# A two-layer decoder trunk in split fp32: normalisation of the second half of queries and keys without priority, three raw weight buffers in place of four, transposes of the attention two matmuls further apart

## The chip, the cores and the metric

The kernel runs on one core of one Trainium2 chip. The metric is the device time of one execution in microseconds (us); lower is better. Traces are of one profiled execution each.

In what follows PE is the matmul engine (its weight loads are listed as PEld), DVE the vector engine, ACT the scalar engine, POOL the general engine, and SP the engine that here only issues transfers. The work of one engine runs in the order in which its instructions stand in its stream. The transfers that SP issues stand in one queue as well: an instruction of SP that waits holds back all later ones.

## The reference

Input is x, 512 tokens by 2048 columns in fp32. Two residual layers follow, each `x <- x + W_out(mixer(rms_norm(x)) * silu(gate))`, both with one wide input projection.

```python
# layer 0: differential attention, 8 heads, each with 2 x 128 query and key columns, 256 value columns
q, k, v, gate = split(rms_norm(x) @ w_in)
q, k = rope(rms_norm(q, q_gain)), rope(rms_norm(k, k_gain))
p = softmax(where(causal, q @ k.T * dh ** -0.5, neg))     # for both halves of a head
o = (p[0] - lam * p[1]) @ v
out = (rms_norm(o, subln_w) * (1 - lambda_init) * silu(gate)) @ w_out

# layer 1: RWKV-7, 32 heads of 64 columns, r, k, v, gate, decay and in-context rate a from one projection
S = S * w_t + (S @ a_t) b_t^T + v_t k_t^T                 # along the 512 tokens
y_t = S @ r_t                                            # then group norm, gate, w_out
```

## The kernel before

Every large product is computed as three products of halves: `split_w` makes from a raw fp32 weight tile a rounded part `wh` (a cast on ACT, line 105) and the rest `wl` (a subtraction on DVE, line 106), and the activations lie as `hH` and `hL`. A raw tile is 128 partitions by two row blocks of 512 columns, 512 KB. It is loaded by SP (line 78) into the pool `wraw` of four buffers that rotate; the pools `wh` and `wl` have two buffers each.

**Layer 0.** Head 0 projects its 1024 columns plainly. Heads 1 to 7 go through `unit_head`, which computes the 2 x 2 block product of a head by seven block products on sums of blocks, in groups of 12 matmuls of 512 columns (line 565), one raw tile for a group. A product has four groups. Four of the raw tiles of a head lie in tiles of their own, `Ta` to `Td`, and are loaded by `first_tiles` while the head before still runs; the other four come through `load` (line 545) into `wraw`, first the lower rows of the query and key columns, then those of the value columns. POOL adds other quarters of the weights to these tiles by accumulating transfers (`add_w`).

When a head's projections for a half of the tokens are there, `head_qk` treats the query and key columns of two token tiles: squares on ACT (line 261), then on DVE two rotary products (269, 270), the sum of squares (271), the cosine product (272), the sum (273), at the end of both tiles the inverse root (274 and lines 64 to 71), and the scaling of the keys by four small ACT instructions (line 280). `take` (line 527) adds a product to what is accumulated. The transposes into `qkT` and `qkL` follow on PE (`turn_qk`, line 295). The half [0, 1] comes in the middle of a head. The half [2, 3] comes at its end and stands inside `high_priority(offset=AHEAD)`.

Attention of head h-1 runs among the matmuls of head h. A `Chain` is a generator; each yielded number says after how many matmuls its next step is put in (`tick`). `attention` yields 8 after scores and weighing, and gap - 8 after transposes: `turn` transposes the probabilities (line 363), `turn_y` transposes the head's output into `yTh` and `yTl` (line 400), which ACT's queue stores to `ys` for the output projection. For head 0 a chain of its own transposes the queries and keys, with a delay of 104 matmuls.

**Layer 1.** There are 16 pairs of heads with one pattern. For each pair k, gate, r and v are projected (two raw tiles each, 24 matmuls a tile, line 122), and two small matrices come into `upw`, a ninth tile of the pool `wraw` (lines 1565 and 1566), split into `sHup` (1098) and `sLup` (1099). A triangular solve on DVE (lines 1353 and 1355) gives `Tm`, POOL stores it to `td` (1357), SP reads it back rearranged into `TT` by four transfers (line 1370), DVE transposes it (1379), and the `px` matmuls (1385, 1395) and the Gram matmuls (1288) follow on PE. The scan of the pair before runs between the projection matmuls.

**Who sets the order.** A tile scheduler places each engine's instructions by priority, the order of the program with the offsets of `high_priority`; `split_w` is itself urgent. Waits come from the data and from the rotation of buffers. A load into `wraw` waits until the `wl` of that buffer's last user has been computed.

Of the kernel before, what the change touches and what calls it, by code (L numbers as in the profile page):

```python
# [57 lines left out]
def rsqrt(g, out, v, n, tag):  # L58

    nc = g.nc  # L60
    m = 1 if tag in ("r4", "r16") else 2
    sh = g.small.tile([P, n], I32, name="rs_i", tag=tag + "i", bufs=m)
    t = g.small.tile([P, n], F32, name="rs_t", tag=tag + "t", bufs=m)
    nc.vector.tensor_single_scalar(sh[:], v.bitcast(I32), 1, ALU.logical_shift_right)
    nc.vector.tensor_scalar(sh[:], sh[:], -1.0, float(0x5F3759DF), ALU.mult, ALU.add)
    y = sh[:].bitcast(F32)
    for i in range(3):
        nc.vector.tensor_mul(t[:], y, y)
        nc.vector.scalar_tensor_tensor(t[:], t[:], -0.5, v, ALU.mult, ALU.mult)
        o = out if i == 2 else y  # L70
        nc.vector.scalar_tensor_tensor(o, t[:], 1.5, y, ALU.add, ALU.mult)
# [254 lines left out]
def attention(g, h, qkT, qkL, sq, V, VL, G, gap, rows=None, keys=()):  # L326
# [87 lines left out]
    for i in range(NT + 3):  # L414
        if i > 1 and i < NT + 2:
            weigh(i - 2)
        if i > 2:
            turn_y(i - 3)
        if i < NT + 2:
            yield 8  # L420
        while due:
            store(*due.pop())
        if i == NT + 2:
            break
        if 0 < i <= NT:
            turn(i - 1)
        if i < NT:
            scores(i)
        if i == 0 and keys:
            yield 7  # L430
            turn_qk(*keys[0])
            yield 9
            turn_qk(*keys[1])
            yield max(gap - 24, 6)
        else:
            yield gap - 8
    if rows is not None:
        rows += last

# [90 lines left out]
def unit_head(g, aps, h, t1s, sq, turned):  # L530


    nc = g.nc
    c1, c2 = qk_cols(aps, h), vg_cols(aps, h)
    acc1 = g.work.tile([P, 2, 512], F32, name="acc1", tag="acc1", bufs=1)
    acc = [None, None, acc1[:, 0], acc1[:, 1]]
    q = [t[:] for t in t1s]
    N = NH4 // KG
    last = h == NH - 1

    def pair():
        return [g.pp.tile([P, 512], F32, name="pp", tag="pp") for _ in range(2)]

    def load(k0, parts):
        raw = g.wraw.tile([P, KG, 512], F32, name="wraw", tag="wraw")
        load_w(g, raw, parts, k0, slice(0, KG))
        return raw

    def split(raw):
        return split_w(g, None, KG, 512, 0, raw)  # L550

    def block(k0, t0):
        return lambda k, t: [x[k0 + k][:, t0 + t * P : t0 + (t + 1) * P] for x in (g.hH, g.hL)]

    def form(nm, i):
        return lambda k, t: [x[:, t * P : (t + 1) * P] for x in g.sums[nm][i * KG + k]]

    def products(out, lhs, raw, start=False, end=False):
        wt = split(raw)
        for t in range(2):  # L560
            first = start
            for lo in range(2):
                for k in range(KG):
                    for x in lhs(k, t)[: 2 - lo]:
                        m = nc.tensor.matmul(out[t][:], x, wt[lo][:, k, :], start=first, stop=end and lo == 1 and k == KG - 1,  # L565
                                             skip_group_check=True)
                        tick(g, m)
                        first = False

    def all_groups(out, lhs, raw, start=False, end=False, then=None):  # L570
        for i in range(N):
            r = raw(i)
            products(out, lhs(i), r, start and i == 0, end and i == N - 1)
            if then:
                add_w(g, r, then[0], then[1] + i * KG)

    def s4(out, keep, start=False, end=False):
        def raw(i):
            keep.append(load(NH4 + i * KG, c2))
            return keep[-1]  # L580
        all_groups(out, lambda i: form("S4", i), raw, start, end, None if last else (c2, 0))

    chained = lambda i: g.Ts[i]
    y = pair()
    all_groups(y, lambda i: block(NH4 + i * KG, 0), lambda i: load(NH4 + i * KG, c1), True, True)
    copy_out(g, q[:2], y)
    y = pair()
    all_groups(y, lambda i: block(i * KG, 0), chained, True, False, (c2, 0))
    take(g, q[:2], y)
    X = pair()  # L590
    all_groups(X, lambda i: form("S1", i), chained, True, last, (c2, NH4))
    copy_out(g, acc[2:], X)
    b22 = []
    if not last:
        s4(X, b22, end=True)
        G, acc[:2] = gates(g)
        copy_out(g, acc[:2], X)
    all_groups(y, lambda i: form("S2", i), chained, then=(c1, NH4))
    if last:
        G, acc[:2] = gates(g)  # L600
    take(g, acc[:2], y, ALU.subtract, acc[2:] if last else None)

    def square():
        X = pair()
        all_groups(X, lambda i: block(NH4 + i * KG, 256), chained, True, True)
        return X

    def third():
        for i in range(N):
            if last:  # L610
                b22.append(load(NH4 + i * KG, c2))
                add_w(g, b22[i], c2, i * KG)
            products(y, form("S3", i), b22[i], end=i == N - 1)
        take(g, acc[2:], y, ALU.subtract)

    head_qk(g, t1s, sq, [0, 1])
    if last:
        copy_out(g, q[2:], square())
        third()
        take(g, q[2:], y)  # L620
        with g.tc.high_priority(offset=AHEAD):
            head_qk(g, t1s, sq, [2, 3])
        turned()
        X = pair()
        s4(X, [], True, True)
        take(g, acc[:2], X)
        return head_vg(g, h, acc, G)
    turned()
    third()
    copy_out(g, q[2:], y)  # L630
    values = head_vg(g, h, acc, G)
    X = square()
    first_tiles(g, aps, h + 1)
    take(g, q[2:], X)
    with g.tc.high_priority(offset=AHEAD):
        head_qk(g, t1s, sq, [2, 3])
    return values


# [154 lines left out]
def layer0(g, aps):  # L794
# [3 lines left out]
    with ExitStack() as cx:  # L798
# [25 lines left out]
        with tc.high_priority(offset=AHEAD):  # L824
# [4 lines left out]
                first = nc.scalar.dma_start(out=g.prm_a[:], in_=aps["norm_w"]).ins  # L829
            g.last = load_w(g, g.first[0][0], qk_cols(aps, 0), 0, slice(0, 1), nc.sync)  # L830
            warmed = warm_up(10)
            on = g.const.tile([P, 1], F32, name="on")
            nc.vector.memset(on[:], 0.0)
            with tc.issue_after(first):
                nc.scalar.copy(on[:], on[:])
# [17 lines left out]
        g.last = None  # L853
        t1s = [t1_tile() for _ in range(NT)]
        copied = copy_out(g, [t[:] for t in t1s], qk0)
        sc = g.small.tile([P, NT, 4], F32, name="ssc", tag="ssc", bufs=1)
        for cb, tags in enumerate((("qkL",), ("sA2",), ("sC2",), ("qkL",))):
            n = NT // len(tags)
            xs = []
# [30 lines left out]
        for h in range(NH):  # L890
# [6 lines left out]
            def keys(n, t1s=t1s, qkT=qkT):  # L897
                for t in range(n):
                    turn_qk(g, t1s, *qkT, t)
                    if t < n - 1:  # L900
                        yield 20
# [4 lines left out]
            else:  # L906
                for ts in ([0, 1], [2, 3]):
                    head_qk(g, t1s, sq, ts)
                Chain(g, keys(NT), 104)
                input_sums(g, pairs, False)  # L910
                ps = unit_tok(g, g.hH, g.hL, vg_cols(aps, h), 512)
                acc1 = g.work.tile([P, 2, 512], F32, name="acc1", tag="acc1", bufs=1)
# [70 lines left out]
        def banks(i):  # L983
            if i < 2:
# [1 line left out]
            return [g.ps.tile([P, 512], F32, name="z", tag="pa", bufs=2) for _ in range(2)]  # L986

        T2 = g.work.tile([P, KG, 512], F32, name="T2", tag="Tb", bufs=1)
        load = loader(g, aps["da_w_out"], ((g.wraw, "wraw", 4), (g.work, "V", 1), (g.wraw, "wraw", 4),
                                              (g.work, "G", 1), (g.wraw, "wraw", 4)))  # L990

        rs = g.small.tile([P, NT], F32, name="rs1", tag="ss")
        ss = g.small.tile([P, NT], F32, name="ss1", tag="rr")
# [217 lines left out]
def stage1(g, j, k, up):  # L1211
# [14 lines left out]
    lw, tha = th  # L1226
    nc.scalar.activation(lw[:], lw[:], AF.Identity, bias=g.hdec[:], scale=-0.5 * DECAY)
    l = w.tile([P, NC_, C], F32, name="l", tag="l", bufs=1)
    m = g.small.tile([P, NC_], F32, name="m", tag="m")
    p.E = w.tile([P, NC_, C + 1], F32, name="E", tag="E", bufs=1)  # L1230
    p.gam = g.small.tile([P, NC_], F32, name="gam", tag="gam", bufs=3)
    p.AR = w.tile([P, NC_, 2, C], F32, name="AR", tag="AR", bufs=3)
# [281 lines left out]
def centre(g, p):  # L1514

    nc, w, Y = g.nc, g.work, p.Y
    s1 = g.small.tile([P, NT, 2], F32, name="s1", tag="s1")
    p.yc = w.tile([P, 2 * NT, C], F32, name="yc", tag="yc", bufs=1)
    for h in range(2):
        yg = Y[h][:, : NT * C].rearrange("p (t n) -> p t n", t=NT)  # L1520
# [6 lines left out]
def group_norm(g, j, p):  # L1527
# [2 lines left out]
    NG = 2 * NT  # L1530
    sq = w.tile([P, NG, C], F32, name="ysq", tag="thg", bufs=1)
    nc.scalar.activation(sq[:], yc[:], AF.Square)
    var = g.small.tile([P, NG], F32, name="var", tag="var")
    nc.vector.reduce_sum(var[:], sq[:], AX.X)
    nc.vector.tensor_scalar(var[:], var[:], 1.0 / C, GN_EPS, ALU.mult, ALU.add)
    rs = g.small.tile([P, NG], F32, name="rsg", tag="rsg")
    rsqrt(g, rs[:], var[:], NG, "r8")
    nc.vector.tensor_mul(yc[:], yc[:], rs[:, :, None].to_broadcast([P, NG, C]))

# [10 lines left out]
def layer1(g, aps):  # L1550
    nc, tc = g.nc, g.tc
    with ExitStack() as cx:
# [127 lines left out]
        def banks(i):  # L1680
            if i == 0:
# [4 lines left out]
        load = loader(g, aps["rw_w_out"], ((g.wraw, "wraw", 4), (w, "G1", 2), (g.wraw, "wraw", 4), (w, "LT", 1),  # L1686
                                              (g.wraw, "wraw", 4), (w, "G1", 2)))
        seven(g, aps["rw_w_out"], load, rows, sums, 2, 3, acc, Ts, banks, done)


# [1 line left out]
def body(ctx, tc, nc, aps):  # L1692
# [3 lines left out]
    g.chains, g.later, g.state = [], [], None  # L1696
    g.const = ctx.enter_context(tc.tile_pool(name="const", bufs=1))
    g.hp = ctx.enter_context(tc.tile_pool(name="hp", bufs=16))
    g.wraw = ctx.enter_context(tc.tile_pool(name="wrawp", bufs=4))
    g.wh = ctx.enter_context(tc.tile_pool(name="whp", bufs=2))  # L1700
    g.wl = ctx.enter_context(tc.tile_pool(name="wlp", bufs=2))
    g.small = ctx.enter_context(tc.tile_pool(name="small", bufs=2))
# [53 lines left out]
```

## Time and profile before

| what | us |
|---|---|
| median of three runs | 2172.89 |
| the three runs | 2160.70, 2172.89, 2174.74 |
| profiled execution, its time | 2171.03 |
| profiled execution, its span | 2169.3 |
| PE busy | 2110.7 |
| DVE busy | 1614.6 |
| ACT busy | 1149.3 |

The span runs from the first to the last instruction of the trace. Layer 0 with its output projection takes roughly the first half, up to about 1000 us, layer 1 the rest. All times inside the trace are from the start of the span. The mean granted PE clock of the profiled execution is 0.984 of full speed.

### The profile page before, as it was taken

What the parts mean: (1) busy time and instruction counts of PE and PEld (TensorE: products, weight loads), DVE (VectorE), ACT (ScalarE), POOL (GpSimd) and SP (SyncE); (2) the same over time, 40 slices, a digit from 0 to 9 for tenths busy, and PEclk for the clock granted to TensorE, in tenths of its full rate; (3) what the DMA queues carried; (4) which work ended last, traced back from release to release, by engine and by line L of the source; (5) the groups of instructions that cost most, each with busy time, mean ns of one, the idle gap of its engine ahead of it and who ended that gap; (6) DMA issues with size and microseconds to landing.
All of it is one profiled execution on the core that took longest, in us unless ns stands there. A gap on an engine that the chain in (4) does not pass through costs nothing.

```text
span 2169.3 us, 34050 instructions
## 1 busy us (share of the span) xinstructions
PE 2110.7 (97%) x11852; PEld 1711.5 (79%) x11852; DVE 1614.6 (74%) x4129; ACT 1149.3 (53%) x2278; POOL 386.2 (18%) x751
## 2 busy tenths in 40 slices
PE   9999999999998999999899999999999999999999
PEld 7787878778787788878677778888887888867887
DVE  6887888888787885566777667877776788757644
ACT  5665656566565543355554555565555555545322
POOL 1020111201113000101322222222222122221001
PEclk9999999999999999999998999999999999999999
DMA  8487877879789836623222322322332233335555
GB/s 271 131 173 186 181 159 182 163 180 178 165 186 213 300 112 184 140 87 103 77 74 63 93 81 83 91 89 78 101 102 84 82 92 90 108 111 185 179 156 120
DMA packets 143102, 294.60 MB, mean 136 GB/s; under 512 B 47969, under 2 KB 65377, under 8 KB 142929
## 3 DMA queue, kind: packets, MB, share of 16 engines
q1 hardware_dynamic: 75072, 178.55, 25.8%
q0 software_dynamic: 25216, 87.74, 21.9%
q10 hardware_dynamic: 42640, 26.14, 4.0%
q8 instruction: 93, 1.52, 0.3%
q14 instruction: 81, 0.66, 0.1%
HBM read 268.71 MB, written 23.66 MB: 135 GB/s over the span
## 4 chain that ended last, share of the span: by engine, by line
PE 49%; DVE 14%; DMA 5%; issue 3%; ACT 2%; POOL 0%; SPq 0%; ACTq 0%; POOLq 0%; DVEq 0%
PE pp L122 29%; PE pt L122 5%; PE pp L565 3%; DVE wl L106 3%; DVE tmpl L1353 2%; DMA td<-Tm 2%; DVE Tm L1355 2%; PE gp L1288 2%; DMA TT<-td 1%; PE sm L1466 1%; PE sm L1477 1%; PE px L1395 1%; PE lora L122 1%; PE px L1385 1%; ACT wh L105 1%
## 5 line engine op out<-in xcount | busy, mean ns | idle before, releaser
L106 DVE TENSOR_TENSOR wl<-wraw,wh 128x1024 fp32r<-128x1024 f32 (+2 forms) x291 | 356.1, 1224 | 230.5 <-ACT wh L105 222.3
L105 ACT CAST wh<-wraw 128x1024 fp32r<-128x1024 f32 (+2 forms) x291 | 303.5, 1043 | 328.1 <-PE pp L122 153.5
L122 PE MATMUL pp<-hH,wl 128*128 128x512 f32 x1024 | 417.4, 408 | 0.2 <-DVE wl L106 0.2
L122 PE MATMUL pp<-hL,wh 128*128 128x512 f32 x1024 | 416.3, 407 | 0.0
L122 PE MATMUL pp<-hH,wh 128*128 128x512 f32 x1024 | 415.5, 406 | 0.0
L122 PEld LDWEIGHTS pp<-hH,wh 128*128 128x128 f32 x1024 | 196.0, 191 | 36.6 <-issue 2.7
L122 PEld LDWEIGHTS pp<-hL,wh 128*128 128x128 f32 x1024 | 195.8, 191 | 35.7
L122 PEld LDWEIGHTS pp<-hH,wl 128*128 128x128 f32 x1024 | 195.4, 191 | 33.9 <-DVE wl L106 0.7
L565 PE MATMUL pp<-wh,hH 128*128 128x512 f32 x448 | 176.7, 394 | 0.1
L565 PE MATMUL pp<-wh,hL 128*128 128x512 f32 x448 | 175.8, 392 | 0.0
L565 PE MATMUL pp<-wl,hH 128*128 128x512 f32 x448 | 142.2, 397 | 9.4 <-DVE wl L106 9.4
L122 PE MATMUL pp<-wh,hH 128*128 128x512 f32 x372 | 145.8, 392 | 0.9 <-ACT hH L1089 0.9
L122 PE MATMUL pp<-wl,hH 128*128 128x512 f32 x372 | 146.0, 393 | 0.4 <-DVE wl L106 0.4
L122 PE MATMUL pp<-wh,hL 128*128 128x512 f32 x372 | 145.6, 391 | 0.1
L1472 POOL COPY SA<-VS 64x64 f32<-64x64 f32 x224 | 64.5, 288 | 450.3 <-DVE VS L1488 349.7
L1353 DVE SCALAR_TENSOR_TENSOR tmpl<-LT,Tm 128x60 f32<-128x60 f32 (+24 forms) x496 | 134.5, 271 | 11.5
L1355 DVE TENSOR_TENSOR Tm<-Tm,tmpl 128x60 f32<-128x60 f32 (+24 forms) x496 | 104.0, 210 | 10.6
L565 PEld LDWEIGHTS pp<-wl,hH 128*128 128x128 f32 x448 | 82.5, 189 | 27.8 <-DVE wl L106 11.9
L565 PEld LDWEIGHTS pp<-wh,hH 128*128 128x128 f32 x448 | 84.6, 189 | 17.7 <-issue 0.5
L565 PEld LDWEIGHTS pp<-wh,hL 128*128 128x128 f32 x448 | 84.5, 189 | 17.3
L1469 ACT COPY rhs<-sm 64x64 f32<-64x64 f32 x256 | 52.5, 205 | 74.6 <-PE sm L1466 71.9
L1479 ACT COPY VS<-sm 64x64 f32<-64x64 f32 x256 | 52.7, 206 | 59.5 <-PE sm L1477 54.0
(394 smaller groups left out, 4493.8 us busy)
## 6 DMA issues: line engine op xcount, KB each, us to landing
wraw<-in_rw_w_in_dram SPq DMA_DIRECT2D x128, 512.0 KB
wraw<-in_da_w_in_dram SPq DMA_DIRECT2D x75, 512.0 KB
wraw<-in_da_w_in_dram POOLq DMA_DIRECT2D x28, 512.0 KB, 5.8
wraw<-in_da_w_out_dram SPq DMA_DIRECT2D x26, 512.0 KB
wraw<-in_rw_w_out_dram SPq DMA_DIRECT2D x26, 512.0 KB
Ta<-in_da_w_in_dram POOLq DMA_DIRECT2D x21, 512.0 KB, 5.6
Tb<-in_da_w_in_dram POOLq DMA_DIRECT2D x21, 512.0 KB, 5.7
Tc<-in_da_w_in_dram POOLq DMA_DIRECT2D x21, 512.0 KB, 6.0
```

Of the source, the lines that this page charges most:

```text
L105: a = nc.scalar.copy(hi[:, ks], raw[:, ks])
L106: d = nc.vector.tensor_sub(lo[:, ks], raw[:, ks], hi[:, ks].bitcast(F32))
L122: m = nc.tensor.matmul(out, a, b, start=s, stop=e, skip_group_check=skip)
L565: m = nc.tensor.matmul(out[t][:], x, wt[lo][:, k, :], start=first, stop=end and lo == 1 and k == KG - 1, skip_group_check=True)
L1288: m = nc.tensor.matmul(gp[h][:, i * P : (i + 1) * P], BK[r_, c0 + i, :, :], p.AR[r_, c0 + i, :, :], start=True, stop=True)
L1353: nc.vector.scalar_tensor_tensor(tt, LT[:, i : i + 1, i + 1 :].to_broadcast([P, s, n]), n2[:, i : i + 1], Tm[:, 0:s, i : i + 1].to_broadca ...
L1355: nc.vector.tensor_add(Tm[:, 0:s, i + 1 :], Tm[:, 0:s, i + 1 :], tt)
L1385: nc.tensor.matmul(px[hi, c * HALF : (c + 1) * HALF], p.G[lo, c, 0, h, HALF:C], T1[lo, c, :], start=True, stop=True, tile_position=(b0, b0 ...
L1395: nc.tensor.matmul(px[lo, N + c * HALF : N + (c + 1) * HALF], X[hi, c, :], TT[hi, c, h, HALF:C], start=True, stop=True, tile_position=(b0 ...
L1469: nc.scalar.copy(rhs[r_, :], sm[r_, h * C : h * C + C])
L1472: nc.gpsimd.tensor_copy(p.SA[r_, c - 1, :], VS[r_, c, h, :])
L1479: nc.scalar.copy(VS[r_, c, h, :], sm[r_, P : P + C])
```

## The change

There are three parts. First, the two calls of `head_qk` for the half [2, 3] lose `high_priority(offset=AHEAD)`. Second, `wraw` has three buffers in place of four; in heads 1 to 7 of layer 0 the fourth load of a product goes to a tile `Te` of its own, so that four tiles rotate there as before. The output projections, the low-rank tiles and layer 1 have three. Some small tiles get a third buffer or another place; the room comes from the buffer that is gone. Third, `attention` yields 10 where it yielded 8, and takes two from the following gap, so that a round is as long as before; the first gap has a floor of 6 and stays at 6. The chain of head 0's keys starts after 120 matmuls in place of 104.

```diff
 def rsqrt(g, out, v, n, tag):
-    m = 1 if tag in ("r4", "r16") else 2
+    m = 1 if tag in ("r4", "r16") else 3 if tag == "r8" else 2
...
         if i < NT + 2:
-            yield 8
+            yield 10
...
             turn_qk(*keys[1])
-            yield max(gap - 24, 6)
+            yield max(gap - 26, 6)
         else:
-            yield gap - 8
+            yield gap - 10
...
-    def load(k0, parts):
-        raw = g.wraw.tile([P, KG, 512], F32, name="wraw", tag="wraw")
-        load_w(g, raw, parts, k0, slice(0, KG))
+    def load(i, k0, parts):
+        pool, tag, bufs = (g.work, "Te", 1) if i == N - 1 else (g.wraw, "wraw", 3)
+        raw = pool.tile([P, KG, 512], F32, name="wraw", tag=tag, bufs=bufs)
+        load_w(g, raw, parts, k0 + i * KG, slice(0, KG))
         return raw
...
         third()
         take(g, q[2:], y)
-        with g.tc.high_priority(offset=AHEAD):
-            head_qk(g, t1s, sq, [2, 3])
+        head_qk(g, t1s, sq, [2, 3])
         turned()
...
     take(g, q[2:], X)
-    with g.tc.high_priority(offset=AHEAD):
-        head_qk(g, t1s, sq, [2, 3])
+    head_qk(g, t1s, sq, [2, 3])
     return values
...
-            on = g.const.tile([P, 1], F32, name="on")
+            on = g.small.tile([P, 1], F32, name="on", tag="so")
...
-        sc = g.small.tile([P, NT, 4], F32, name="ssc", tag="ssc", bufs=1)
+        sc = g.work.tile([P, NT, 4], F32, name="ssc", tag="y", bufs=1)
...
-                Chain(g, keys(NT), 104)
+                Chain(g, keys(NT), 120)
...
-        load = loader(g, aps["da_w_out"], ((g.wraw, "wraw", 4), (g.work, "V", 1), (g.wraw, "wraw", 4),
-                                              (g.work, "G", 1), (g.wraw, "wraw", 4)))
+        load = loader(g, aps["da_w_out"], ((g.wraw, "wraw", 3), (g.work, "V", 1), (g.wraw, "wraw", 3),
+                                              (g.work, "G", 1), (g.wraw, "wraw", 3)))
...
-    g.wraw = ctx.enter_context(tc.tile_pool(name="wrawp", bufs=4))
+    g.wraw = ctx.enter_context(tc.tile_pool(name="wrawp", bufs=3))
```

The tiles `m`, `s1`, `var` and `rsg` of layer 1 get `bufs=3`, and the loader of `rw_w_out` names three buffers in the same way.

More of the change, by code (lines that the diff above doesn't have):

```diff
@@ L578, in raw @@
         def raw(i):
-            keep.append(load(NH4 + i * KG, c2))
+            keep.append(load(i, NH4, c2))
             return keep[-1]
@@ L584, in unit_head @@
     y = pair()
-    all_groups(y, lambda i: block(NH4 + i * KG, 0), lambda i: load(NH4 + i * KG, c1), True, True)
+    all_groups(y, lambda i: block(NH4 + i * KG, 0), lambda i: load(i, NH4, c1), True, True)
     copy_out(g, q[:2], y)
@@ L610, in third @@
             if last:
-                b22.append(load(NH4 + i * KG, c2))
+                b22.append(load(i, NH4, c2))
                 add_w(g, b22[i], c2, i * KG)
@@ L1228, in stage1 @@
     l = w.tile([P, NC_, C], F32, name="l", tag="l", bufs=1)
-    m = g.small.tile([P, NC_], F32, name="m", tag="m")
+    m = g.small.tile([P, NC_], F32, name="m", tag="m", bufs=3)
     p.E = w.tile([P, NC_, C + 1], F32, name="E", tag="E", bufs=1)
@@ L1516, in centre @@
     nc, w, Y = g.nc, g.work, p.Y
-    s1 = g.small.tile([P, NT, 2], F32, name="s1", tag="s1")
+    s1 = g.small.tile([P, NT, 2], F32, name="s1", tag="s1", bufs=3)
     p.yc = w.tile([P, 2 * NT, C], F32, name="yc", tag="yc", bufs=1)
@@ L1532, in group_norm @@
     nc.scalar.activation(sq[:], yc[:], AF.Square)
-    var = g.small.tile([P, NG], F32, name="var", tag="var")
+    var = g.small.tile([P, NG], F32, name="var", tag="var", bufs=3)
     nc.vector.reduce_sum(var[:], sq[:], AX.X)
     nc.vector.tensor_scalar(var[:], var[:], 1.0 / C, GN_EPS, ALU.mult, ALU.add)
-    rs = g.small.tile([P, NG], F32, name="rsg", tag="rsg")
+    rs = g.small.tile([P, NG], F32, name="rsg", tag="rsg", bufs=3)
     rsqrt(g, rs[:], var[:], NG, "r8")
@@ L1685, in layer1 @@
         Ts = [flat(x) for x in g.TT] + [w.tile([P, KG, 512], F32, name="T2", tag="BK", bufs=1)]
-        load = loader(g, aps["rw_w_out"], ((g.wraw, "wraw", 4), (w, "G1", 2), (g.wraw, "wraw", 4), (w, "LT", 1),
-                                              (g.wraw, "wraw", 4), (w, "G1", 2)))
+        load = loader(g, aps["rw_w_out"], ((g.wraw, "wraw", 3), (w, "G1", 2), (g.wraw, "wraw", 3), (w, "LT", 1),
+                                              (g.wraw, "wraw", 3), (w, "G1", 2)))
         seven(g, aps["rw_w_out"], load, rows, sums, 2, 3, acc, Ts, banks, done)
```

## The prediction

> **What bounds the kernel now.** I read the page first, then PE's waits, then the timeline around the longest of them, then the granted clock by stretches.
>
> ```profile
> span 2169.3 us, 34050 instructions
> PE 2110.7 (97%) x11852; PEld 1711.5 (79%) x11852; DVE 1614.6 (74%) x4129; ACT 1149.3 (53%) x2278; POOL 386.2 (18%) x751
> L106 DVE TENSOR_TENSOR wl<-wraw,wh 128x1024 fp32r<-128x1024 f32 (+2 forms) x291 | 356.1, 1224 | 230.5 <-ACT wh L105 222.3
> L565 PE MATMUL pp<-wl,hH 128*128 128x512 f32 x448 | 142.2, 397 | 9.4 <-DVE wl L106 9.4
> ```
>
> PE is busy for 97% of the span. It is idle for 2169.3 - 2110.7 = 58.6 us, and only that idle time, and time at a lowered clock, can be won by moving instructions. The last row is a quarter of the answer: the matmuls of `unit_head` sit idle 9.4 us ahead of `wl` and for nothing else. The view of waits puts names to the rest (columns: engine and line, waited for, us in total, times, longest):
>
> ```profile
> PE px L1385 <- DVE T L1379: 14.9, 15, 3.2
> PE pp L565 <- DVE wl L106: 12.1, 7, 2.7
> PE pt L363 <- DVE yTl L400: 3.5, 3, 2.2
> PE pt L295 <- ACT t L280: 3.4, 1, 3.4
> DVE T L1379 <- DMA TT<-td: 24.1, 19, 4.0
> ```
>
> The second, third and fourth rows are layer 0 and are what the change touches. The first and last are layer 1's loop of solve, store, reload and transpose; the change comes near it through the queue of SP.
>
> **First part: the weight split goes ahead of the normalisation.** One boundary of heads, from the timeline (start, length, engine, operation, idle time before):
>
> ```profile
> 281.67 1.23 DVE L106 TENSOR_TENSOR wl<-wraw,wh 128x1024 fp32r<-128x1024 f32 x1 [1.50 <-ACT wh L105]
> 282.81 0.68 DVE L527 TENSOR_TENSOR t<-t,pp 128x512 f32<-128x512 f32 x1
> 283.31 1.05 ACT L105 CAST wh<-wraw 128x1024 fp32r<-128x1024 f32 x1 [1.67 <-PE pp L565]
> 285.83 0.61 PE L565 MATMUL pp<-wl,hH 128*128 128x512 f32 x2
> ...
> 288.47 0.16 DVE L274 TENSOR_SCALAR ss<-ss 128x8 f32<-128x8 f32 x1
> 288.54 1.22 DVE L106 TENSOR_TENSOR wl<-wraw,wh 128x1024 fp32r<-128x1024 f32 x1
> 289.82 1.20 PE L565 MATMUL pp<-wl,hH 128*128 128x512 f32 x4 [1.56 <-DVE wl L106]
> 290.35 1.22 DVE L106 TENSOR_TENSOR wl<-wraw,wh 128x1024 fp32r<-128x1024 f32 x1
> 295.76 1.28 ACT L280 ACTIVATE t<-t,rr 128x128 f32<-128x128 f32 x4
> ```
>
> ACT has the cast ready at 283.31 + 1.05 = 284.36, but DVE works through twelve operations of `take` and `head_qk` from 282.81 to 288.54 before it subtracts. PE meanwhile puts off the `wl` matmuls of the group, does all others, and stands for 1.56 us. In the built order of the changed kernel the next `wl` stands after three of the twelve operations. They take some 1.7 us from 282.81, so it starts at about 284.5 and ends at 285.7. PE needs it one step of 1.36 us (half a group of 12 matmuls) after the pair at 285.83, at 287.2: covered by 1.5 us. The second new place comes after three further operations (285.7 + 1.6 + 1.2 = 288.5, needed 1.36 x 2 later than the first, 289.9), the third after five (about 291.8, needed 292.6). So the wait goes, six times 1.56 us; 6 x 1.56 = 9.4 is the idle time in the L565 row above. The seventh is the last head:
>
> ```profile
> 741.56 1.20 PE L565 MATMUL pp<-wl,sumdd1H 128*128 128x512 f32 x4 [2.69 <-DVE wl L106]
> ```
>
> The same exchange is made there. 9.36 + 2.69 = 12.05 us, the 12.1 of the waits.
>
> What is late next: the normalisation now ends later by about three splits on DVE. The scaling L280, at 295.76 here, moves to about 298.0 and, cut by casts, ends at about 300.3. PE's transposes of token tile 2 need it at 300.7 (they stand at 302.24 in the timeline, less the 1.56 us that PE is earlier). The slack is 0.4 us: I cost it at nothing, its upper bound is the first rival. The matmuls that step back to their ordinary places cost nothing, they are the same in number.
>
> **Second part: the attention's transposes, +2 matmuls.** The waits on `yTl`:
>
> ```profile
> 691.72 0.55 PE L363 MATMUL pt<-ident,a 128*128 128x128 f32 x3 [1.03 <-DVE yTl L400]
> 702.34 0.35 DVE L400 SCALAR_TENSOR_TENSOR yTl<-yt,subw,yTh 128x128 fp32r<-128x128 f32 x1 [2.13 <-DMA ys<-yTl]
> 703.07 1.12 PE L363 MATMUL pt<-ident,a 128*128 128x128 f32 x4 [2.15 <-DVE yTl L400]
> ```
>
> Both stand in the attention of head 6. In the built order `turn` comes two to four matmuls of 512 columns later; a step of six takes 1.36 us, so two are 0.45 us and four 0.9. The wait at 691.72 then nearly goes (0.9 of 1.03). The one at 703.07 does not come from PE's place: `yTl` itself waits for the store before it, 2.13 us, in the stretch where transfers take the whole of the engines (below). Only two matmuls go from it, 0.45 us. I take 1.4 us; bounds 0 (the store lands that much later, since it is issued later) and 3.2.
>
> Head 0's keys: the delay 104 to 120 moves no transpose in PE's built order, so the 3.4 us of L295 stays. Value 0, bounds 0 and 3.4.
>
> **Third part: three buffers.** In heads 1 to 7 the tile `Te` keeps four in rotation, and costs one load at the start, 0.5 MB earlier than needed. Elsewhere a load is issued one user later. A pair of layer 1:
>
> ```profile
> 1578.99 7.21 SPq L78 DMA_DIRECT2D wraw<-in_rw_w_in_dram  x3
> 1589.03 1.01 POOL L1357 DMA_DIRECT2D td<-Tm  x1 [3.06 <-DVE s L1521]
> 1592.07 1.82 SPq L1370 DMA_DIRECT2D TT<-td  x4
> 1593.79 0.43 DVE L1379 STREAM_TRANSPOSE T<-TT 64x256 f32<-64x256 f32 x1 [0.73 <-DMA TT<-td]
> 1594.28 0.69 PE L1385 MATMUL px<-T,G 32*32 32x32 f32 x16 [0.65 <-DVE T L1379]
> 1600.94 1.05 ACT L105 CAST wh<-wraw 128x1024 fp32r<-128x1024 f32 x1
> 1532.86 0.69 PE L1385 MATMUL px<-T,G 32*32 32x32 f32 x16 [0.64 <-DVE T L1379]
> ```
>
> The tile issued at 1578.99 is cast at 1600.94, 22 us later. Nine tiles share the pool in 1594.28 - 1532.86 = 61.4 us, one each 6.8 us; one buffer less leaves 22 - 6.8 = 15 us for a transfer, far more than it takes. So no weight comes late. In the built order PE's stream in layer 1 is the same instruction by instruction, and POOL's nearly. On SP the small `upw` loads move from the release by one `wl` to the next, and ahead of the `TT` reload stand two weight loads after `upw` where three stood; the last is issued at the same release as the third before, some 1586. The third is issued behind `TT`, where the next already was. So the collision with the reload is as it was, in all pairs but one early one, in which a load waits for `sLup` and then starts close ahead of `TT`. I give that pair 1 us: bounds 0 and a whole transfer of 512 KB, which at the 305 GB/s of a row below is 1.7 us.
>
> **Clock.** The stretches with their granted clock (third figure from the end; before it each engine's busy time):
>
> ```profile
> 700.00:705.00 5.00, 2.85 (x12) 2.15 (x11) 2.80 (x11) 1.57 (x3) 1.92 (x4) 0.79 1.01 244
> 705.00:710.00 5.00, 5.00 (x21) 3.86 (x20) 3.16 (x9) 1.60 (x2) 1.20 (x2) 0.87 0.96 226
> 741.00:750.00 9.00, 8.44 (x39) 6.95 (x40) 8.61 (x20) 4.40 (x6) 0.00 (x0) 1.00 0.89 305
> 1100.00:1571.00 471.00, 459.71 (x3061) 371.73 (x3061) 348.38 (x970) 261.69 (x592) 119.20 (x273) 0.97 0.29 85
> 1280.00:1285.00 5.00, 4.49 (x78) 4.06 (x79) 0.88 (x2) 3.42 (x7) 0.00 (x0) 0.82 0.42 123
> 1285.00:1290.00 5.00, 5.00 (x30) 3.78 (x27) 0.00 (x0) 3.00 (x6) 1.77 (x2) 0.50 0.04 7
> 1590.00:1595.00 5.00, 4.35 (x34) 3.34 (x34) 3.76 (x6) 1.10 (x3) 0.76 (x6) 1.00 0.32 52
> 1634.00:2079.00 445.00, 437.12 (x2808) 353.29 (x2807) 314.15 (x811) 218.98 (x481) 92.00 (x212) 0.97 0.39 118
> ```
>
> The 2.69 us stand in the last head cost no clock (1.00); the 2.15 us stand at 703 was followed by 0.21 x 5 + 0.13 x 5 = 1.7 us of lost clock. By this row that loss stays as long as most of the stand does, so I add nothing for it. In layer 1 one pair has its `px` wait followed by half clock (1280 to 1290: 0.18 x 5 + 0.5 x 5 = 3.4 us lost), another (1594) has the same wait and full clock. The two long rows lose 0.03 x 916 = 27 us, as much as eight such dips.
>
> The Trainium skill (TensorE: Matmul & The Clock Gate, Part 1) says that the clock falls to half after an idle window of about 3.4 us. By that rule alone none of the stands removed here, at most 2.69 us, would carry clock with it, and the sum stays as it is; the trace agrees at 741 and not at 703 or 1280, where 2.15 and 0.82 us of idle time came with half clock, so I go by the rows.
>
> **Sum.** -12.05 - 1.4 + 1.0 = -12.5 us on the profiled 2171.03 us: 2158.6 us. The profiled execution lies 1.9 us under the median 2172.89, so the prediction is 2160.4 us.
>
> **Rivals.** *A new wait on the scaled keys.* Against it are 0.4 us of computed slack, for it that ACT's casts now cut L280. The nearest rows are the 0.65 us of the `px` wait at 1594, where an operand is just late, and the 3.4 us of L295 on L280 in head 0. I take 0.8, near the first, since the order puts the need only just after the end: 0.8 x 7 = 5.6 us, 2166.
>
> *The dips of layer 1 fall otherwise.* Layer 1 begins 12 us earlier, and whether a `px` wait drops the clock differs between pairs with equal waits. Four dips less are 4 x 3.4 = 13.6 us: 2147, and if the stand at 703 goes with its clock, a little less. Four more: 2174. The runs of before spread over 14 us, which is about four dips. The page named above calls the gate's window free-running; no run here shows the window itself.
>
> *The reload queues behind a weight load.* SP works in order, and with three buffers its loads are released later. From the point where the last release slips by more than 1592.07 - 1586.2 - 1.7 = 4.2 us, `TT` stands behind 512 KB in every pair: 15 waits x 1.7 = 25.5 us, and the longer waits would drop the clock in the 15 - 8 = 7 pairs that keep it now, 7 x 3.4 = 24: 2160 + 49 = 2209. For it: `T` already waits on `TT` 24.1 us in all. Against: the order above. The Trainium skill (DMA: Bandwidth & Descriptors, Queues, rings and completion order) says that each ring consumes descriptors in order, which speaks for this rival: a reload cannot pass a load ahead of it. That no load comes ahead of it that was not there is what the order says.
>
> *The change does not do what it says:* another engine's wait takes the 12 us at once, for instance since ACT's casts are freed by PE. No row shows one; 2172.
>
> **How the numbers follow.** Forecast 0.50 (2153 to 2168), scaled keys 0.13 (2166), fewer dips 0.14 (2147), more dips 0.08 (2174), no effect 0.05 (2172), reload 0.10 (2209). A change of 1%, 21.7 us, is about what a measurement can tell from none. Under 2151 lies only the case of fewer dips: faster 0.14; slower is the reload: 0.10; the rest 0.76. The range 2146 to 2175 leaves out the reload and the outer half of the dips.
>
> **What would show it.** Right: no idle time ahead of L565 for `wl`, at six boundaries and in the last head; L363's wait near 2 us; L295's 3.4 us as before; in layer 1 equal `px` waits with the dips in other pairs. Wrong: a wait of L295 on L280 at each boundary; `T` waiting on `TT` for more than 2 us in steady pairs; a cast in layer 1 that waits for a transfer.

## The result and the profile after

The changed kernel takes 2150.89 us in the median of ten runs (2145.62 to 2160.05), the kernel before beside it 2168.45 us (2156.13 to 2174.74). The ratio is 0.993, 95% interval 0.9904 to 0.9956. A second series gave 0.9942 (0.9921 to 0.9963). The forecast was 2160.4 / 2172.89 = 0.9943.

The profiled execution of the changed kernel, first rows of its page and the group that had idled for `wl` (line 566 is the old 565):

```profile
span 2152.2 us, 34019 instructions
PE 2104.0 (98%) x11852; PEld 1706.3 (79%) x11852; DVE 1613.1 (75%) x4129; ACT 1153.1 (54%) x2278; POOL 386.0 (18%) x751
L566 PE MATMUL pp<-wl,hH 128*128 128x512 f32 x448 | 140.6, 393 | 0.1
```

The 9.4 us of idle time ahead of this group are 0.1. PE's idle time in all went from 58.6 to 2152.2 - 2104.0 = 48.2 us. Its waits, in the view of waits (engine and line, waited for, us in total, times, longest):

```profile
PE px L1384 <- DVE T L1378: 14.0, 16, 3.5
PE pt L295 <- DVE qkL L299: 5.3, 7, 1.0
PE pt L295 <- ACT t L280: 4.3, 3, 3.4
PE pt L363 <- DVE yTl L400: 1.0, 1, 1.0
```

No row for `wl` in the heads is left. The second row has grown; in the kernel before it was this:

```profile
PE pt L295 <- DVE qkL L299: 1.9, 7, 0.7
```

The new places of the splits can be read at the same boundary as in the prediction. DVE in the changed kernel:

```profile
282.88 1.23 DVE L106 TENSOR_TENSOR wl<-wraw,wh 128x1024 fp32r<-128x1024 f32 x1 [1.50 <-ACT wh L105]
...
285.68 1.22 DVE L106 TENSOR_TENSOR wl<-wraw,wh 128x1024 fp32r<-128x1024 f32 x1
...
288.65 1.22 DVE L106 TENSOR_TENSOR wl<-wraw,wh 128x1024 fp32r<-128x1024 f32 x1 [0.22 <-ACT wh L105]
...
291.66 1.22 DVE L106 TENSOR_TENSOR wl<-wraw,wh 128x1024 fp32r<-128x1024 f32 x1
```

The first stands 1.21 us later than in the trace before (head 1 begins later in this execution). Less that, the three that were moved start at 284.5, 287.4 and 290.5, where the prediction's sums give 284.5, 287.3 and 290.6.

Executions of one kernel differ by several us, mostly because their granted clocks do. A measure with less scatter is the time at full clock: a run's time multiplied by its mean granted clock. Below, its mean over the runs of a kernel stands against that of the kernel before in the same series (2138 to 2139 us), with one standard error of the difference; what the clock took is given beside it. The clock of a run is on record to 0.001, which is 2 us, and the errors contain that. Kernels of different series are compared by their differences to the kernel before. The second series of the changed kernel has -8.5 +- 0.7 us at full clock, and the clock took 3.7 +- 2.0 us less than before.

### The profile page after: what moved, and what is told of

Read it like the earlier page. It is cut to its first block, busy times and chain, and to the rows that moved or that the text cites. A ratio compares the mean times of both kernels' runs of the same rounds, so it can differ in the third digit from the quotient of the medians.

```text
span 2152.2 us, 34019 instructions
## 1 busy us (share of the span) xinstructions
PE 2104.0 (98%) x11852; PEld 1706.3 (79%) x11852; DVE 1613.1 (75%) x4129; ACT 1153.1 (54%) x2278; POOL 386.0 (18%) x751
## 4 chain that ended last, share of the span: by engine, by line
PE 36%; DVE 9%; DMA 3%; issue 2%; ACT 1%; POOL 0%; ACTq 0%; SPq 0%; DVEq 0%; POOLq 0%
PE pp L122 22%; PE pt L122 5%; DMA td<-Tm 2%; DVE tmpl L1352 2%; DVE wl L106 2%; DVE Tm L1354 1%; PE gp L1287 1%; PE sm L1465 1%; DMA TT<-td 1%; PE sm L1476 1%; PE sm L1483 1%; PE px L1384 1%; PE px L1394 1%; DVE VS L1487 1%; PE pt L1207 0%
## 5 line engine op out<-in xcount | busy, mean ns | idle before, releaser
L1352 DVE SCALAR_TENSOR_TENSOR tmpl<-LT,Tm 128x60 f32<-128x60 f32 (+24 forms) x496 | 135.0, 272 | 11.6
```

What stands on the lines that cost most here:

```text
L1352: nc.vector.scalar_tensor_tensor(tt, LT[:, i : i + 1, i + 1 :].to_broadcast([P, s, n]), n2[:, i : i + 1], Tm[:, 0:s, i : i + 1].to_broadca ...
```

## The experiments

**The parts one by one.** First the priority alone, on the kernel before.

```diff
-        with g.tc.high_priority(offset=AHEAD):
-            head_qk(g, t1s, sq, [2, 3])
+        head_qk(g, t1s, sq, [2, 3])
```

> The kernel before with only the priority of the second half's normalisation taken away. Theory (the split stalls are what layer 0 wins, and the new 0.7 to 1.0 us waits of the key transposes come from the later scaling): no wait of the matmuls on the weight rest at the seven boundaries, the key transposes wait about 0.5 us more at each, L363 still waits about 3 us with its clock loss; the output projection of layer 0 begins 8 to 9 us earlier than before; in all 0.994 to 0.998 of before, with the layer 1 part within its scatter. Rival A (the new waits of the key transposes come from the wider spacing of the attention): they stay at 0.2 us here and layer 0 wins 11 to 12 us. Rival B (layer 1's gain comes with the shift of its start against the clock's window): fewer half-clock stretches here than before too, with the px waits in steady pairs still at 0.65 us.

Measured: 0.9971 (0.9948 to 0.9995); at full clock -9.0 +- 0.6 us, as the theory had it: 12.1 us of waits for `wl`, less what the key transposes wait longer. Its waits:

```profile
PE pt L295 <- DVE qkL L299: 5.7, 7, 0.9
```

The wait on `wl` is gone, and the wait of the key transposes is there already, without the spacing. So rival A falls: the spacing is not needed for this wait. The clock took 3.1 +- 2.3 us more than before, not less, which speaks against rival B.

Then the spacing alone.

```diff
-            yield 8
+            yield 10
...
-            yield max(gap - 24, 6)
+            yield max(gap - 26, 6)
...
-            yield gap - 8
+            yield gap - 10
...
-                Chain(g, keys(NT), 104)
+                Chain(g, keys(NT), 120)
```

> The kernel before with only the attention's transposes two matmuls further apart and the keys' delay of 120. Theory: L363's waits fall from 3.5 to about 1 us and the clock loss at 703 goes, 2.5 to 4 us in all; the six waits of 1.56 us stay; ratio 0.997 to 1.000. Rival A: the key transposes after a boundary wait 0.7 us and more here, which takes back 3 us: ratio about 1.000.

Measured: 0.9995 (0.9977 to 1.0012), at full clock -0.6 +- 0.7 us. The theory had L363 at about 1 us and 2.5 to 4 us in all, and missed. L363 still waits:

```profile
PE pt L363 <- DVE yTl L400: 1.7, 1, 1.7
PE pt L363 <- DVE qkL L299: 1.2, 1, 1.2
```

That is 2.9 us in this execution. Before, it was 3.5 us on `yTl` and this:

```profile
PE pt L363 <- DVE qkL L299: 0.4, 1, 0.4
```

In the traces of kernels without the spacing these two waits of L363 come to 1.7 to 3.9 us together, in those with it to 0 to 3.4 us. So the 2.5 us that the trace of the changed kernel shows as won on `yTl` are mostly the scatter of one execution. Rival A falls here too: the key transposes have one wait on `qkL`, of 0.7 us.

Then the third part alone: three buffers, `Te`, the small tiles.

```diff
-        raw = g.wraw.tile([P, KG, 512], F32, name="wraw", tag="wraw")
+        pool, tag, bufs = (g.work, "Te", 1) if i == N - 1 else (g.wraw, "wraw", 3)
+        raw = pool.tile([P, KG, 512], F32, name="wraw", tag=tag, bufs=bufs)
...
-    g.wraw = ctx.enter_context(tc.tile_pool(name="wrawp", bufs=4))
+    g.wraw = ctx.enter_context(tc.tile_pool(name="wrawp", bufs=3))
```

> The kernel before with only the third part: three raw buffers, the tile Te, the small tiles. Theory C (with three buffers one weight load less overlaps the store of the solved triangles): in the steady pairs of layer 1 the store lands 0.2 us earlier, the px wait is about 0.54 us in place of 0.65, the clock falls in fewer pairs, and layer 1 wins 4 to 8 us; the start of layer 0 loses about 1 us: ratio 0.996 to 0.999. Rival B (phase against the clock's window alone): px waits 0.54 us as well, but as many half-clock stretches as before, clock 0.984, ratio 1.000 to 1.002. One early pair loses 1 to 2 us in both.

Measured: 1.0005 (0.9991 to 1.002), at full clock +1.9 +- 0.7 us. The signs of theory C are there in the trace, the store of the triangles lands 0.2 us earlier. The view of transfers has it in one row (issuing queue, count, size, median us from issue to landing), first the changed kernel's, then that of priority alone, which has the place of the kernel before:

```profile
td<-Tm POOLq DMA_DIRECT2D x16, 128.0 KB, 2.8
```

```profile
td<-Tm POOLq DMA_DIRECT2D x16, 128.0 KB, 3.0
```

The gain of theory C did not come with it: the time did not fall. The ratio is the one of rival B, but the clock took as much as before (-0.4 +- 1.7 us).

The parts add up within their errors: -9.0 - 0.6 + 1.9 = -7.7 us at full clock, against the whole with -8.5 +- 0.7.

**The whole again, and without the spacing.** The changed kernel as it is, and the changed kernel with the yields and the delay of the kernel before.

> The changed kernel once more, beside the parts on one chip. Priority alone came to 0.9971, spacing alone to 0.9995, buffers alone to 1.0005. If the parts add up, the whole is 0.997; if layer 1 keeps the clock in the steady pairs only with three buffers and layer 0 gains by the parts together, it is 0.993 to 0.995 as first measured. Steady pairs: the px wait 0.53 to 0.6 us, the triangles' store lands 4.2 us after the solve, no half clock in most of them.

> The changed kernel without the wider spacing: priority and buffers alone. If the spacing adds nothing of its own (alone 0.9995), this equals the changed kernel within 0.1%, and L363 waits 1 to 3 us more, with the wait on qkL at the last head's boundary as in the run of priority alone (1.4 us). If the spacing matters only once the split stalls are gone, this is 2 to 4 us slower than the changed kernel.

Measured: 0.9942 (0.9921 to 0.9963) and 0.9957 (0.9938 to 0.9976); at full clock -8.5 +- 0.7 and -7.7 +- 0.9. In ratios the parts do not add up, 0.997 against 0.9942. What lies between is mostly clock: priority alone lost 3.1 +- 2.3 us more to it than the kernel before, the whole 3.7 +- 2.0 us less. The intervals of the two runs overlap; the spacing is worth 0.8 +- 1.1 us here.

**A fourth raw tile in layer 1.** If the store lands earlier because one weight load less runs beside it, a fourth tile must take that back.

```diff
+def raw_tile(g, shape, name):
+    n = getattr(g, "turns", None)
+    if n is None:
+        return g.wraw.tile(shape, F32, name=name, tag="wraw")
+    g.turns = n + 1
+    if n % 4 == 3:
+        return g.work.tile(shape, F32, name=name, tag="Te", bufs=1)
+    return g.wraw.tile(shape, F32, name=name, tag="wraw")
...
+        g.turns = 0
         begin(0)
```

> The changed kernel with a fourth raw tile in rotation in layer 1 (a tile Te of layer 1's own, every fourth raw tile goes there). Theory (one weight load less overlaps the store of the triangles with three buffers): in steady pairs the store lands 4.4 us after the solve in place of 4.2, the px wait is 0.65 in place of 0.55, half clock comes back in some of the steady pairs, the early pairs lose their extra wait; the time is within 3 us of the changed kernel's or up to 6 us over it. Rival (the gap between the landing times has another cause, the shift of layer 1): 4.2 us and the px wait 0.55 as in the changed kernel.

Measured: 0.9917 (0.9884 to 0.995); at full clock -10.0 +- 1.0 us, 1.5 +- 1.2 us better than three buffers. The loads stood as before the change, three of them between `upw` and the reload, and yet:

```profile
td<-Tm POOLq DMA_DIRECT2D x16, 128.0 KB, 2.8
```

So theory C fell, and the shift of layer 1 could not be it either, since the kernels with priority or spacing alone are shifted as well and have 3.0. What the kernels with 2.8 share, and those with 3.0 lack, is the place of the tile `Tm`. `Tm` holds the solved triangles that the store takes. In the built programs it starts at byte 191008 of each partition before the change (32 modulo 256), at 187008 after it (128 modulo 256), and at 191104 with the fourth tile (again 128).

**The place alone.** An unused tile of 96 bytes in the kernel before, one of 160 bytes in the changed kernel, each ahead of layer 1's work tiles.

```diff
         g.lc = cx.enter_context(tc.tile_pool(name="lc1", bufs=1))
+        pad = g.lc.tile([P, 24], F32, name="pad")    # 40 in the changed kernel
+        nc.gpsimd.memset(pad[:], 0.0)
```

> The kernel before with one unused tile of 96 bytes per partition ahead of layer 1's work tiles, and one memset of it; nothing else. It moves the solved triangles Tm from byte 191008 (32 modulo 256) to 191104 (128 modulo 256), where every kernel with the third part has them. Theory (the third part quickens their store by its place alone, not by its buffers): the store's packets take 0.73 us in place of 1.0, it lands 4.2 us after the solve in place of 4.39, the px wait in steady pairs is 0.53 to 0.6 in place of 0.65 to 0.8, 1 to 3 us in all, more where the clock is kept: ratio 0.997 to 1.000. Rival (other small tiles or the order of the third part do it): 4.39 as before.

> The changed kernel with one unused tile of 160 bytes at the same place, so that Tm lies at 32 modulo 256 as in the kernel before. Theory: the store lands 4.39 us after the solve in place of 4.2, the px waits grow by 0.1 us or more in steady pairs, 1 to 3 us in all and some half-clock stretches more: 0.995 to 0.998 of before, where the changed kernel has 0.994. Rival: 4.2 us as in the changed kernel.

Measured: the kernel before with 96 bytes more has 0.9973 (0.9955 to 0.9992), at full clock -3.9 +- 0.6 us. The changed kernel with `Tm` back at 32 modulo 256 has 0.9973 (0.9955 to 0.9991), at full clock -6.6 +- 0.7 where it had -8.5. One steady pair of the kernel with 96 bytes, the store, the reload and the matmuls behind it:

```profile
1583.56 1.01 POOL L1357 DMA_DIRECT2D td<-Tm  x1 [3.09 <-DVE s L1521]
1586.43 1.82 SPq L1370 DMA_DIRECT2D TT<-td  x4
1588.82 0.69 PE L1385 MATMUL px<-T,G 32*32 32x32 f32 x16 [0.65 <-DVE T L1379]
```

and of the changed kernel with 160 bytes:

```profile
1579.25 1.01 POOL L1356 DMA_DIRECT2D td<-Tm  x1 [3.09 <-DVE s L1520]
1582.32 2.02 SPq L1369 DMA_DIRECT2D TT<-td  x4
1584.77 0.69 PE L1384 MATMUL px<-T,G 32*32 32x32 f32 x16 [0.95 <-DVE T L1378]
```

From the issue of the store to that of the reload it is 2.87 us in the first and 3.07 in the second; the prediction's rows of the kernel before have 3.04. Most pairs show the same: of the sixteen, eleven have 3.04 to 3.06 us in the kernel before and 2.85 to 2.87 with the 96 bytes; nine have 3.04 to 3.07 with the 160 bytes and 2.85 to 2.88 in the changed kernel without them. The others are longer: those at the ends, and in the last two kernels two between. Order and buffers of the first are those of the kernel before. So the place decides the 0.2 us. Sixteen times 0.2 us is 3.2, near the 3.9 +- 0.6 measured. The other tiles of layer 1 move with `Tm`; whether one of them has a share was not tried. In the changed kernel the place is worth 1.9 +- 1.0 us.

The clock may go with it. The same stretches of steady pairs, granted clock third from the end, first the kernel before, then the one with 96 bytes:

```profile
1280.00:1590.00 310.00, 305.73 (x2079) 250.36 (x2080) 233.11 (x646) 172.41 (x389) 76.83 (x175) 0.98 0.30 89
1590.00:1880.00 290.00, 285.49 (x1938) 234.12 (x1937) 214.63 (x582) 162.24 (x364) 72.49 (x170) 0.98 0.31 89
```

```profile
1280.00:1590.00 310.00, 306.13 (x2128) 250.33 (x2126) 238.48 (x654) 173.78 (x391) 78.27 (x185) 1.00 0.31 91
1590.00:1880.00 290.00, 287.11 (x1961) 235.69 (x1958) 222.59 (x608) 168.03 (x380) 75.12 (x170) 1.00 0.32 93
```

In slices of 5 us from 1260 to 1900 us, the granted clock falls under 0.9 in three to five places in each of the four traces with 3.0 us (the kernel before, priority alone, spacing alone, 160 bytes), and in none to three in each of the ten with 2.8. Over the runs the clock took 2.7 +- 1.6 us less with the 96 bytes. The changed kernel with 160 bytes lost 0.9 +- 1.8 us more to it than the kernel before, the changed kernel 3.7 +- 2.0 us less. That is the same direction both times, at less than two standard errors each.

**The wait that came new.** Three matmuls more between the two key transposes.

```diff
-            yield 9
+            yield 12
             turn_qk(*keys[1])
-            yield max(gap - 26, 6)
+            yield max(gap - 29, 6)
```

> The changed kernel with the second of the two key transposes three matmuls later (yield 12 in place of 9 between them). If the 0.7 to 1.0 us wait at each boundary is the second transpose standing too close behind the first, whose DVE part is held up by a weight split, the wait goes from 5.3 us in all to under 2, and the time falls by 3 to 4 us against the changed kernel: 0.991 of before. If the wait only moves with the transpose or the later transposes of the attention collide, 0.993 as the changed kernel.

Measured: 0.9933 (0.9916 to 0.9951), 2147.5 us. The ratio is not the 0.991 that was expected, and its interval overlaps with that of the changed kernel. At full clock it is -12.1 +- 0.9, 3.6 +- 1.1 us better than the changed kernel. In its trace a wait of 1.3 us on `rs_i` is new at L363. The wait on `qkL` is down to one of 0.7 us:

```profile
PE pt L295 <- DVE qkL L299: 0.7, 1, 0.7
```

Here is why it was there. In the changed kernel, at the boundary shown above:

```profile
299.98 0.99 ACT L280 ACTIVATE t<-t,rr 128x128 f32<-128x128 f32 x3
302.02 0.60 PE L295 MATMUL pt<-ident,t 128*128 128x128 f32 x4
303.81 1.23 DVE L106 TENSOR_TENSOR wl<-Td,wh 128x1024 fp32r<-128x1024 f32 x1
304.95 0.68 DVE L299 TENSOR_TENSOR qkL<-pt,qkT 128x512 fp32r<-128x512 f32 x1
305.69 0.66 PE L295 MATMUL pt<-ident,t 128*128 128x128 f32 x4 [1.00 <-DVE qkL L299]
```

The keys are scaled at 300.97 and the first transpose does not wait for them. The second waits until `qkL` of the first is made (both are written to the tile `pt` of one PSUM tag, which has to be read out first), and `qkL` stands on DVE behind the split of `Td`. In the kernel before:

```profile
302.24 0.60 PE L295 MATMUL pt<-ident,t 128*128 128x128 f32 x4
303.62 1.23 DVE L106 TENSOR_TENSOR wl<-Td,wh 128x1024 fp32r<-128x1024 f32 x1
304.76 0.68 DVE L299 TENSOR_TENSOR qkL<-pt,qkT 128x512 fp32r<-128x512 f32 x1
305.59 0.63 PE L295 MATMUL pt<-ident,t 128*128 128x128 f32 x4 [0.21 <-DVE qkL L299]
```

And with priority alone:

```profile
301.14 0.60 PE L295 MATMUL pt<-ident,t 128*128 128x128 f32 x4
303.13 1.23 DVE L106 TENSOR_TENSOR wl<-Td,wh 128x1024 fp32r<-128x1024 f32 x1
305.10 0.63 PE L295 MATMUL pt<-ident,t 128*128 128x128 f32 x4 [0.82 <-DVE qkL L299]
```

DVE's chain takes the same time in all three (1.8 us from the start of the split to the end of `qkL`). In the kernel before it begins 1.38 us behind the first transpose, with priority alone 1.99 us behind it: without the stand for `wl` PE is early against DVE by 0.61 us, which is what the wait has grown by. In the changed kernel the chain begins 1.79 us behind, and PE has nine matmuls between the two transposes where both other traces have eleven, 0.46 us less at 0.23 us a matmul. So at this boundary about half of the wait that is new in the changed kernel comes from the place of the transposes.

**Head 0, and a better kernel.** Three versions on top of the later transpose: priority for the normalisation of head 0, both halves; the fourth raw tile in layer 1; the fourth tile and priority for head 0's second half alone. The edit to head 0 in the last of them:

```diff
-                for ts in ([0, 1], [2, 3]):
-                    head_qk(g, t1s, sq, ts)
+                head_qk(g, t1s, sq, [0, 1])
+                with tc.high_priority(offset=AHEAD):
+                    head_qk(g, t1s, sq, [2, 3])
```

> The changed kernel with the second key transpose three matmuls later and the normalisation of head 0 given the priority that the second halves lost. If head 0's 3.4 us wait of the key transposes on the scaled keys comes from its normalisation standing behind layer 1's constants and the sums of weights on the vector engine, it shrinks to under 1.5 us with the clock loss of about 1.7 us behind it, and the time is 3 to 5 us under the run with the later transpose alone (2147.5): about 0.991 of before. If the splits that now wait behind the normalisation take it back, as they did at the boundaries before, 0.993.

> The changed kernel with the second key transpose three matmuls later and the fourth raw tile of layer 1. Their gains by themselves in time at full clock were 2.3 and 1.5 us against the changed kernel. If they add, 3.8 us under the changed kernel: 0.991 to 0.993 of before.

> As the run with later transpose and fourth raw tile, and with priority for the second half of head 0's normalisation alone, between whose operations the splits stand in the order. If the 3.4 us wait on head 0's scaled keys goes without the 2.2 us wait on a split that the priority for both halves brought: 2 to 4 us less than without it, 0.990 to 0.991 of before.

Measured: 0.9926 (0.9899 to 0.9953), 0.9932 (0.9908 to 0.9955) and 0.9901 (0.9869 to 0.9932); at full clock -12.1 +- 0.6, -11.6 +- 0.9 and -13.3 +- 0.6 us. Priority for both halves moved the wait: the 3.4 us on the keys went, and a wait of 2.2 us on a split came in their place.

```profile
PE pp L122 <- DVE wl L106: 2.8, 3, 2.2
```

The fourth tile added nothing to the later transpose that these runs can show (-11.6 against -12.1). The last version is the fastest, 2143.73 us against 2165.0 for the kernel before in its series; at full clock it is 4.8 +- 0.9 us better than the changed kernel, though the intervals of the ratios overlap. It has the ratio that was expected, but not for the reason given: the clock took 8.8 +- 3.2 us less than before. Its 3.4 us wait in head 0 became one of 3.0 us on a copy out of PSUM (`copy_out`, 259 there):

```profile
PE pp L577 <- ACT acc L259: 3.0, 1, 3.0
```

so its gain over the run with the later transpose alone, 1.2 +- 1.1 us at full clock, cannot be told from none.

## Why the prediction was right, point by point

- *The split stalls, -12.05 us: right in place and size.* The wait on `wl` is gone at all seven boundaries, and at the boundary shown the splits stand to 0.2 us where the sum had put them.
- *"What is late next ... I cost it at nothing": this step failed in size.* The scaled keys were in time, as computed (scaled at 300.97, transposed at 302.02 without a wait). The step looked at the first transpose alone. The second waits for DVE's half of the first, over the seven boundaries 5.3 us in place of 1.9, which gave back 3.4 us; moving it away won 3.6 +- 1.1 us. The rival on the scaled keys had a price not far off (5.6 us) but the wrong operand.
- *The spacing, -1.4 us: -0.6 +- 0.7 measured alone.* This cannot be told from 0; the 1.4 us are not shown, and 0 was a bound of the term. The wait of 3.4 us on head 0's keys stayed, as forecast.
- *The buffers, 1 us for one early pair: too small.* That pair's loads, store, reload and `px` matmuls in the trace after:

```profile
1198.85 0.83 SPq L78 DMA_DIRECT2D wraw<-in_rw_w_in_dram  x2
1200.20 0.98 POOL L1356 DMA_DIRECT2D td<-Tm  x1 [2.46 <-DVE Tm L1355]
1206.63 1.82 SPq L1369 DMA_DIRECT2D TT<-td  x4
1208.86 0.69 PE L1384 MATMUL px<-T,G 32*32 32x32 f32 x16 [1.00 <-DVE T L1378]
...
1211.10 0.95 PE L1384 MATMUL px<-T,G 32*32 32x32 f32 x16 [1.55 <-DVE T L1378]
```

The same pair in the kernel before:

```profile
1206.19 0.33 SPq L78 DMA_DIRECT2D wraw<-in_rw_w_in_dram  x1
1207.53 0.98 POOL L1357 DMA_DIRECT2D td<-Tm  x1 [1.27 <-DVE Tm L1356]
1212.10 1.82 SPq L1370 DMA_DIRECT2D TT<-td  x4
1216.52 0.69 PE L1385 MATMUL px<-T,G 32*32 32x32 f32 x16 [0.61 <-DVE T L1379]
```

Two loads go out close ahead of the store where one did. From the store to the reload it is 6.4 us in place of 4.6, and PE waits 2.55 us in place of 0.61, so the pair lost 1.9 us, a little over the bound of 1.7. The reload is not held up behind a load, as the rival had it: it waits for the store, which lands late. With the fourth tile this pair is back at 4.6 us. In the steady pairs no such delay came but in two, at 1337 (3.8 us to the reload) and 1707 (3.2 us). The run of priority alone, with four buffers, has 3.7 us in the same two pairs, so these are not the buffers' doing.

The buffers cost more than that pair, though. The third part alone is +1.9 +- 0.7 us at full clock with the favourable place of `Tm`, which is worth 3.9 us in the kernel before and 1.9 in the changed one. If the two add up, the buffers and the rest of that part cost some 4 to 6 us. The fourth tile of layer 1 gave 1.5 +- 1.2 us of it back. Where the remainder lies is open; the start of layer 0, where PE's longest wait for `hH` is 0.9 us in the kernel before and 1.6 in the changed one but 1.2 in a second trace of that, scatters too much for single traces to tell.
- *Not seen at all: the place of `Tm`.* No term of the sum had it: 3.9 +- 0.6 us at full clock in the kernel before, 1.9 +- 1.0 in the changed one, and perhaps some clock. The change moved it by chance.
- *The dips of layer 1.* They are the scatter, as the rival on the dips had it: among the runs of a kernel the loss by the clock has a standard deviation of 2.5 to 7 us, the time at full clock one of 1.1 to 2.7. The prediction called the waits at 1280 and 1594 the same, though they are 0.82 and 0.65 us; still, two pairs of the kernel before have 0.70 us both, at 1345 and at 1410, and only the first has a lowered clock behind it (0.80 in its slice of 5 us, against 1.00). But the dips may not be luck alone: the traces have more of them in the steady pairs where the reload comes 0.2 us later.
- *The clock at 703.* The loss of 1.7 us behind the stand there was expected to stay. In the trace of the changed kernel, where the longest wait of L363 is 1.0 us, the clock is full from 695 to 705.

The forecast 0.9943 against 0.993 and 0.9942 is therefore right in part by luck. At full clock the change is worth 8.5 +- 0.7 us, not the 12.5 of the sum; 3.7 +- 2.0 us of clock, for which the sum had nothing, made up the rest. Within the 8.5, 3.4 us for the transposes and most of 4 to 6 us for the buffers were missing on one side, 2 to 4 us for the place of a tile on the other.

## What to carry to other kernels

After a stall is removed, follow the engine that was waiting to its next meetings with each engine, not only to the next operand that the change delays: PE may now arrive earlier there, and a chain that had just been in time is late. Compare the addresses of stored tiles in the two builds, and where a measured gain has no place in the sum, move the suspected tile by a dummy tile before crediting the edit. Where the clock differs from run to run, multiply each run's time by its granted clock before comparing parts of a change of under one per cent.

## What the runs showed of the hardware

A store of 128 KB from the 128 partitions took 2.8 us to land when its tile started at 128 modulo 256 bytes and 3.0 us at 32 modulo 256 (medians of sixteen stores, in ten traces and in four). Other places were not tried. The tile is stored in runs of 32 floats, 128 bytes. The Trainium skill (DMA: Bandwidth & Descriptors, How a descriptor splits into AXI transactions) says that a transaction has to start at a multiple of 256 bytes. Worked out from that rule, every second run of 128 bytes takes two transactions at 32 modulo 256, and none does at 128; the direction agrees with the 0.2 us, the mechanism itself is not shown by these runs.

The granted clock fell to half behind waits of 0.6 to 0.8 us in layer 1 of the kernel before, where PE runs 32 by 32 matmuls, and stayed full behind a stand of 2.69 us among matmuls of 512 columns. A wait of 0.70 us had full clock behind it at 1410, and one of 0.82 us had 3.4 us of lost clock behind it at 1280, four times itself.
